# One step of a hybrid decoder layer: the attention's query tile, softmax maxima and head norm, written with other instructions

## Chip, cores and metric

The kernel runs on one core of one Trainium2 chip. The metric is the device time of one execution in microseconds, as the median of several runs, lower being better. The engines are called PE (TensorE; PEld are its weight loads), DVE (VectorE), ACT (ScalarE), POOL (GpSimd) and SP (SyncE, used only to issue DMAs).

## The reference, cut to what matters

The layer has two parts that read the same normalised input: differential attention (4 heads, each with two query/key halves of 64 and values of 128) and a gating MLP over chunks of 128 positions. Their results are concatenated, projected and added to the input; then comes a feed-forward network with 4096 hidden channels. It does this for a prompt of 512 tokens and for 8 sequences of 4 new tokens each, which read 4096 cached positions through a page table.

```python
def prompt_diff_attn(q, k, v, lam):          # per block of 128 queries
    s = einsum('bthcd,bshcd->bhcts', q_blk, k) * QK_DIM ** -0.5
    p = softmax(where(causal, s, -inf), axis=-1)
    a = p[:, :, 0] - lam * p[:, :, 1]        # the two halves of a head
    return einsum('bhts,bshd->bthd', a, v)

def merge_out(att, mix, subln_gain, lam_init, w_out):
    o_att = (rms_norm(att, subln_gain) * (1.0 - lam_init)).reshape(B, T, ATT_WIDTH)
    return concatenate([o_att, mix], axis=-1) @ w_out

def sample_diff_attn(q, k_new, v_new, k_past, v_past, lam):
    # the same softmax difference, over 4096 cached positions and the new ones
```

All tensors are fp32. rms_norm divides each row by the root of its mean square and multiplies it with a gain vector; for the attention's result that gain, `subln_gain`, has one entry for each of the 128 value channels and is the same for all heads.

## The kernel before, in words

Tokens lie on partitions in four tiles of 128 (the 32 new tokens are a fifth, small one), or on columns where a matmul needs them so. To keep fp32 accuracy each weight block and each activation is split into a rounded part and the rest (`wh`/`wl`, `Thi`/`Tlo`), and each product is three matmuls. `w_conv` (line 262) splits a weight block: ScalarE rounds, VectorE subtracts; `split` (line 716) does the same for a transposed activation tile.

The work is a main line, with two streams beside it. The main line is `setup`, `in_proj` (line 821: ten column blocks of the input projection), `out_proj` (line 1052) and eight groups of the feed-forward network (`ffn`, line 1141). The first stream is the new tokens' attention over the cache: 64 steps, each with one indirect DMA of keys (`kraw`), a 32x32-block transposition of them on VectorE (`k_tr`, line 557, tile `kt`), scores (`scores`, line 573, PSUM tile `S`), a softmax, transposed probabilities copied out by ScalarE (`ptr`, line 614, tile `PT`) and a product with the cached values (PSUM tile `O`). Eight steps are one sequence, so `scores` starts a new sequence every eighth step. `pump` (line 692) sets these steps out along the main line by costs that the main line reports. The second stream is the prompt's attention, 16 units of (query tile i, head h) in three stages: `attn_a` (line 952) computes scores and the unnormalised difference of the two softmaxes, `attn_b` transposes it, `attn_c` (line 1003) multiplies with the values. Its stages are interleaved with the later column blocks of `in_proj` and the first of `out_proj`.

The order of instructions on an engine isn't quite that of the program: the framework orders them by its own estimates, and the class `Ordered` (line 41) bounds this. In the stretches called `pinned` every engine keeps the program's order. Outside them VectorE and TensorE may move an instruction by up to 28 places, GpSimd not at all, and ScalarE and SP freely. Then each engine runs its list in order.

The places that the change touches:

- `qz_fill` (line 566) fills the tile `qz`, the stationary operand of the new tokens' scores. It has four blocks of 32 partitions, one for each of four positions in a page, and in block q only the columns of q may differ from zero; the rest was set to zero once. It is filled once for a sequence by eight copies of 32x32 out of `qT4`, which lies on partitions 64 to 95 of the tile `rows`. The first matmul of a sequence's scores waits for it, and the next fill waits for the last scores of the sequence before.
- `masks` makes `mh`, a 128x4 tile that is 1 where a partition belongs to block q; it is there before the first fill.
- `attn_a` finds the maximum over the keys of each of the two score tiles, multiplies both maxima with minus 1/8, and takes the exponentials with that bias and a scale of 1/8. `tr_pair` (line 730), which writes the transposed queries, multiplies with a column of the queries' gain out of `gcol`; `finish_piece` (line 746) calls it.
- `attn_c` scales a head's result on ScalarE. After the fourth head it forms the norm's factor on GpSimd, and then multiplies each head's 128x128 block in place with that factor and with `sg`, the gain times 0.8 spread over all partitions.
- `cat_tile` (line 1024) transposes four such blocks, so that channels lie on partitions, and calls `split`.
- `gcols` (line 488) turns a small tile with gain rows into the columns `gcol`; `setup` (line 392) loads its rows through SP.

Of the kernel before, what the change touches and what calls it, by code (L numbers as in the profile page):

```python
# [62 lines left out]
def kernel(  # L63
# [114 lines left out]
    idxK = const.tile([128, NCH], I32, name="idxK")  # L178
    gcol = const.tile([128, 32], F32, name="gcol")
    bhalf = const.tile([128, 4], F32, name="bhalf")  # L180
    wT = const.tile([128, 4, 128], F32, name="wT")
    wTs = const.tile([32, 4, 32], F32, name="wTs")
    bsr = const.tile([32, 20], F32, name="bsr")
# [9 lines left out]
    neglam = const.tile([128, 1], F32, name="neglam")  # L193
    lt = gg[:, 0:256]
    lamsgn = const.tile([64, 1], F32, name="lamsgn")
    qz = const.tile([128, 16, 32], F32, name="qz")

    spk = smp.tile([128, 8, 64], F32R, tag="spk", name="spk")
    cs = []
# [192 lines left out]
    def setup():  # L392
        kt0 = kvp.tile([128, 4096], F32, tag="kt", name="kt0")
        xs = kt0[0:32, 0:1024]
        gm = kvp.tile([128, 1024], F32, tag="pp", name="gm")
        fg = kvp.tile([128, 2048], F32, tag="v", name="fg", bufs=VB)
        junk = kvp.tile([128, 512], F32, tag="om", name="junk")
        ptb = zt_().bitcast(I32).rearrange("p (n q) -> p n q", q=4)
        F = fg[:, 0:896].rearrange("p (f m) -> p f m", f=7)
        gsrc = fg[:, 896:1024]  # L400
        SP.dma_start(out=xs, in_=xs_d)
        SP.dma_start(out=ptb, in_=page_table.rearrange("b l -> (b l)").unsqueeze(0).to_broadcast([128, 256]).rearrange("p (n q) -> p n q", q=4))
        SP.dma_start(out=gm, in_=norm_mix.to_broadcast([128, 1024]))
        w_issue()
        w_issue()
        SP.dma_start(out=xt[0], in_=xp[:, 0, :])
        for o in (1024, 3072):
            w_issue(kt0[:, o:o + 1024].rearrange("p (k c) -> p k c", k=4))
        SP.dma_start(out=qg, in_=q_gain.to_broadcast([128, 64]))
        for t in range(1, 4):  # L410
            SP.dma_start(out=xt[t], in_=xp[:, t, :])

        G.memset(mhalf, -0.5)
        for t in ssb + [cst]:
            G.memset(t, 1.0)
        kw = dict(base=0, channel_multiplier=0, allow_small_or_imprecise_dtypes=True)
        G.iota(pf[:, 7:8], pattern=[[0, 1]], base=0, channel_multiplier=1, allow_small_or_imprecise_dtypes=True)
        make_identity(nc, idt)
        G.iota(F[:, 0].rearrange("p (a b) -> p a b", b=32), pattern=[[0, 4], [1, 32]], **kw)
        G.iota(F[:, 1].rearrange("p (a b) -> p a b", b=32), pattern=[[1, 4], [0, 32]], **kw)  # L420
        G.iota(F[:, 2].rearrange("p (a b) -> p a b", b=8), pattern=[[0, 16], [1, 8]], **kw)
        G.iota(F[:, 3].rearrange("p (a b c) -> p a b c", b=4, c=8), pattern=[[0, 4], [1, 4], [0, 8]], **kw)
        G.iota(F[:, 4].rearrange("p (a b c) -> p a b c", b=8, c=4), pattern=[[0, 4], [1, 8], [0, 4]], **kw)
        G.iota(F[:, 5], pattern=[[1, 128]], **kw)
        G.iota(F[:, 6].rearrange("p (a b) -> p a b", b=4), pattern=[[0, 32], [1, 4]], **kw)
        G.memset(gsrc[0:32, :], 0.0)


        pinned(True)
        for half in range(2):  # L430
            ps = dt_()
            n = 4 if half == 0 else 1
            for i in range(n):
                PE.transpose(ps[:, 128 * i:128 * i + 128], F[:, 4 * half + i], idt)
            V.tensor_copy(out=pf[:, 4 * half:4 * half + n], in_=ps.rearrange("p (f m) -> p f m", f=4)[:, 0:n, 0])

        keep_warm(8)

        x_stat(4, [xs], 32, junk, G)
        xsg = kt0[0:32, 2048:3072]  # L440
        V.tensor_tensor(out=xsg, in0=xs, in1=gm[0:32], op=ALU.mult)
        w_conv()
        ps = dt_()
        for k in range(8):
            PE.transpose(ps[:, 32 * k:32 * k + 32], xsg[:, 128 * k:128 * k + 128], idt[:32, :32])
        keep_warm(5)
        pack(ps[:, 0:256].rearrange("p (k t) -> p k t", k=8), 0, 8)
        w_conv()

        for q in range(4):  # L450
            V.tensor_scalar(out=idxK[32 * q:32 * q + 32, :], in0=ptb[32 * q:32 * q + 32, :, q], scalar1=32.0,
                            scalar2=pf[32 * q:32 * q + 32, 0:1], op0=ALU.mult, op1=ALU.add)
        x_gain(gm, 0)
        for n in range(KB):
            gK(n)
        w_conv()
        SP.dma_start(out=gsrc[0:8, :], in_=norm_mix.rearrange("a (k p) -> (a k) p", p=128))
        SP.dma_start(out=gsrc[8:16, :], in_=norm_ffn.rearrange("a (k p) -> (a k) p", p=128))
        SP.dma_start(out=gsrc[16:20, :], in_=b_spatial.rearrange("a g t -> (a g) t"))
        SP.dma_start(out=gsrc[20:21, 0:64], in_=q_gain)  # L460
        SP.dma_start(out=gsrc[20:21, 64:128], in_=q_gain)
        G.memset(qz, 0.0)
        G.memset(strip, 0.0)
        G.memset(ones, 1.0)
        causal = zt_()[:, 0:128]
        G.memset(causal, 0.0)
        G.affine_select(out=causal, in_=causal, pattern=[[-1, 128]], compare_op=ALU.is_ge, fill=NEG, base=0,
                        channel_multiplier=1)
        G.tensor_copy(out=cab, in_=causal)
        G.tensor_copy(out=idb, in_=idt)  # L470
        return gm, F, gsrc, junk
# [16 lines left out]
    def gcols(gsrc):  # L488
        ps = dt_()
        PE.transpose(ps[:, 0:32], gsrc[0:32, 0:128], idt[:32, :32])  # L490
        V.tensor_copy(out=gcol, in_=ps[:, 0:32])

    def load_params():
        for i, lv in enumerate((lambda_q1, lambda_q2, lambda_k1, lambda_k2)):
# [69 lines left out]
        gK(n + KB)  # L564

    def qz_fill(b):
        for q in range(4):
            for c in range(2):
                V.tensor_copy(
                    out=qz[32 * q:32 * q + 32].rearrange("p (h x e) m -> p h x e m", x=2, e=2)[:, :, c, :, 8 * q + 4 * c:8 * q + 4 * c + 4],  # L570
                    in_=qT4.rearrange("p (h x e) m -> p h x e m", x=2, e=2)[:, :, c, :, 4 * b:4 * b + 4])

    def scores(m):
        b, pj = divmod(m, 4)
        if pj == 0:
            qz_fill(b)
        if pj % 2 == 0:
            Sb[b, pj // 2] = psx.tile([128, 512], F32, tag="S", name="S", bufs=2)
        S = Sb[b, pj // 2]
        kt = ktp.pop(m)  # L580
        for s in range(4):
            for h in range(4):
                mm(S[32 * h:32 * h + 32, 256 * (pj % 2):256 * (pj % 2) + 256].rearrange("p (j x) -> p j x", j=2),
                   qz[:, 4 * h + s, :], kt[:, :, 4 * h + s].rearrange("p j i s -> p j (i s)"), s == 0, s == 3)

    def sm1(b):

# [125 lines left out]
                PE.transpose(ps[:, 128 * k:128 * k + 128], xg[t % 2][:, 128 * kk:128 * kk + 128], idt)  # L713
            split(ps.rearrange("p (k t) -> p k t", k=4), 4 * hf, t)

    def split(psv, k0, t):
        hi = Thi[:, k0:k0 + 4, 128 * t:128 * t + 128]
        A.copy(out=hi, in_=psv)
        V.tensor_tensor(out=Tlo[:, k0:k0 + 4, 128 * t:128 * t + 128], in0=psv, in1=hi, op=ALU.subtract)

    def optB(ps, t, hiw, low, half, first=0):

# [23 lines left out]
    def finish_piece(kind, p, ss, items):  # L746
# [18 lines left out]
        def tr(i):  # L765
            z, n, t = items[i]
            if kind == "g":
                return
            dst = (qT if kind == "q" else kT)[:, 2 * p:2 * p + 2, 128 * t:128 * t + 128] if t < 4 else \
                kTs[:, 2 * p:2 * p + 2, :]  # L770
            tr_pair(z, n, dst, gcol[:, 20:21] if kind == "q" else None)

        later(stat)
        for i in range(len(items)):
# [177 lines left out]
    def attn_a(i, h):  # L952
# [7 lines left out]
        a = st_()  # L960
        P = [tt_(), tt_()]
        for c in range(2):
            V.tensor_reduce(out=a[:, c:c + 1], in_=S[c][:, 0:nk], axis=AX.X, op=ALU.max)
        V.tensor_scalar(out=a[:, 0:2], in0=a[:, 0:2], scalar1=-SCALE, scalar2=None, op0=ALU.mult)
        for c in range(2):
            A.activation(out=P[c][:, 0:nk], in_=S[c][:, 0:nk], func=ACTF.Exp, bias=a[:, c:c + 1], scale=SCALE,
                         accum_out=a[:, 2 + c:3 + c])
        V.reciprocal(out=a[:, 4:6], in_=a[:, 2:4])
        V.scalar_tensor_tensor(out=a[:, 3:4], in0=a[:, 5:6], scalar=neglam, in1=a[:, 2:3], op0=ALU.mult, op1=ALU.mult)
# [33 lines left out]
    def attn_c(i, h):  # L1003
# [11 lines left out]
        if h == 3:  # L1015
            rsqrt(ss[:, 0:4], EPS, 1.0 / 128.0)

            def go():
                for j in range(4):
                    V.scalar_tensor_tensor(out=cat[:, j, :], in0=cat[:, j, :], scalar=ss[:, j:j + 1], in1=sg,  # L1020
                                           op0=ALU.mult, op1=ALU.mult)
            later(go)

    def cat_tile(i, k0s=(0, 4)):

        srcs = [qT[:, k, 128 * i:128 * i + 128] for k in range(4)] + \
            [mix[0][:, i, 128 * k:128 * k + 128] for k in range(4)]
        for k0 in k0s:
            ps = dt_()
            for k in range(4):  # L1030
                PE.transpose(ps[:, 128 * k:128 * k + 128], srcs[k0 + k], idt)
            split(ps.rearrange("p (k t) -> p k t", k=4), k0, i)

    def attention():
        units = [(i, h) for i in range(4) for h in range(4)]
# [370 lines left out]
```

## Time and profile before

| | us |
|---|---|
| median of 3 runs | 833.59 |
| lowest and highest | 831.65, 834.48 |
| the profiled execution | 832.81 |
| its span, first to last instruction | 831.1 |
| PE busy | 804.0 (97%) |
| DVE busy | 545.5 (66%) |
| ACT busy | 357.4 (43%) |
| POOL busy | 187.1 (23%) |

The mean granted clock of PE over the span was 0.986 of full speed. DMAs moved 219.06 MB at 264 GB/s. The first 36 us are setup; the input projection and both attentions fill the time to about 366 us; from there the feed-forward network runs with the rest of the cache stream beside it, to about 600 us, and then alone with the new tokens' part.

A row names the engine, the operation, the tile written and the tiles read, the shape as partitions x elements of a partition, and how often it occurs. "Idle before" is time in which the engine stood still just before these instructions, with the instruction that ended it. Since the ends of matmuls are modelled, a stretch in which PE is busy throughout may still hold small gaps; the share of weight loads (PEld) shows them better. All names have one line, L52, because every operation goes through one helper.

### The profile page before, as it was taken

To read this page: it belongs to the slowest core of one execution; us is meant where nothing else is said; L and a number is where in the kernel's file an instruction comes from. 1 tells how busy PE (TensorE), PEld (TensorE's weight loads), DVE (VectorE), ACT (ScalarE), POOL (GpSimd) and SP (SyncE) were. 2 spreads that over 40 slices of the span, in tenths; PEclk is the share of its full clock that TensorE was granted. 3 is DMA by queue.
4 is the path that set the end of the run, shared out by engine and by line. 5 is a ranking of instruction groups with operands and counts; after the bars stand their busy time and mean duration, and the time that the engine had idled before them with its cause. 6 is when DMAs were issued, how large, how long until landed. Compare 5 with 4: busy or idle time off the path is not lost.

```text
span 831.1 us, 15443 instructions
## 1 busy us (share of the span) xinstructions
PE 804.0 (97%) x6210; PEld 636.0 (77%) x6210; DVE 545.5 (66%) x957; ACT 357.4 (43%) x888; POOL 187.1 (23%) x196
## 2 busy tenths in 40 slices
PE   5899999999899999989999999999999999999997
PEld 5888887766556788876766767666776898998997
DVE  5878866888988954797777676644744534444354
ACT  4544643766563743645154144163332431331231
POOL 4553542254333312222322132120100000000000
PEclk8799999999999999999999999999999999999999
DMA  8597698896978888867989797784597277576202
GB/s 316 194 377 270 229 350 323 301 332 260 366 267 311 339 304 317 324 244 289 337 338 345 290 359 305 259 341 167 171 291 247 80 244 244 172 234 221 76 14 95
DMA packets 101797, 219.06 MB, mean 264 GB/s; under 512 B 6089, under 2 KB 83997, under 8 KB 85341
## 3 DMA queue, kind: packets, MB, share of 16 engines
q0 software_dynamic: 18432, 134.23, 42.1%
q1 hardware_dynamic: 83292, 83.84, 30.7%
q8 instruction: 49, 0.80, 0.4%
q14 instruction: 24, 0.19, 0.1%
HBM read 213.53 MB, written 4.52 MB: 262 GB/s over the span
## 4 chain that ended last, share of the span: by engine, by line
PE 79%; DVE 9%; ACT 6%; DMA 3%; issue 2%; POOL 0%; SPq 0%; DVEq 0%; ACTq 0%
PE d L52 68%; PE O L52 6%; PE S L52 6%; DVE kt L52 3%; ACT PT L52 2%; DMA raw<-in_w_down_dram 1%; DMA kraw<-in_cache_k_dram,idxK 1%; DVE zn L52 1%; DMA raw<-in_w_in_dram 1%; ACT wh L52 1%; DVE Tlo L52 1%; DVE wl L52 1%; ACT t L52 1%; ACT z L52 1%; DVE s L52 1%
## 5 line engine op out<-in xcount | busy, mean ns | idle before, releaser
L52 ACT CAST wh<-raw 128x1024 fp32r<-128x1024 f32 x90 | 94.1, 1048 | 198.5 <-PE d L52 179.0
L52 PE MATMUL d<-a,wh 128*128 128x272 f32 (+1 forms) x704 | 167.0, 341 | 0.0
L52 DVE STREAM_TRANSPOSE kt<-kraw 128x2048 f32<-128x2048 f32 x64 | 146.4, 2297 | 11.2 <-PE S L52 7.7
L52 DVE TENSOR_TENSOR wl<-raw,wh 128x1024 fp32r<-128x1024 f32 x90 | 109.4, 1218 | 57.1 <-ACT wh L52 56.9
L52 PEld LDWEIGHTS d<-a,wh 128*128 128x128 f32 x704 | 113.1, 188 | 24.6 <-issue 5.4
L52 PE MATMUL d<-wh,Thi 128*128 128x256 f32 x432 | 129.0, 299 | 1.8 <-ACT d L52 1.0
L52 POOL DMA_INDIRECT v<-in_cache_v_dram,idxK x64 | 67.0, 1047 | 255.0 <-PE O L52 244.5
L52 PE MATMUL d<-wl,Thi 128*128 128x256 f32 x432 | 123.4, 286 | 0.0
L52 PE MATMUL d<-wh,Tlo 128*128 128x256 f32 x432 | 122.5, 284 | 0.0
L52 PE MATMUL d<-Thi,wh 128*128 128x272 f32 (+2 forms) x368 | 108.7, 336 | 0.0
L52 PE MATMUL d<-Tlo,wh 128*128 128x272 f32 (+2 forms) x368 | 106.5, 330 | 1.4 <-DVE Tlo L52 1.4
L52 PE MATMUL d<-Thi,wl 128*128 128x272 f32 (+2 forms) x368 | 106.4, 329 | 0.0
L52 PE MATMUL d<-a,wl 128*128 128x272 f32 (+1 forms) x352 | 102.8, 336 | 0.0
L52 POOL DMA_INDIRECT kraw<-in_cache_k_dram,idxK x64 | 73.8, 1153 | 110.6 <-DVE kt L52 63.6
L52 PEld LDWEIGHTS d<-wh,Thi 128*128 128x128 f32 x432 | 82.8, 192 | 11.6 <-issue 6.9
L52 PEld LDWEIGHTS d<-wh,Tlo 128*128 128x128 f32 x432 | 82.7, 192 | 0.5 <-issue 0.4
L52 PEld LDWEIGHTS d<-wl,Thi 128*128 128x128 f32 x432 | 82.7, 191 | 0.1
L52 PEld LDWEIGHTS d<-Thi,wh 128*128 128x128 f32 x368 | 63.5, 188 | 18.2 <-issue 7.5
L52 ACT COPY PT<-d 32x128 f32<-32x128 f32 x256 | 65.7, 257 | 14.3 <-DVE d L52 11.1
L52 PEld LDWEIGHTS d<-Tlo,wh 128*128 128x128 f32 x368 | 63.6, 188 | 7.4 <-DVE Tlo L52 1.6
L52 PEld LDWEIGHTS d<-Thi,wl 128*128 128x128 f32 x368 | 63.5, 188 | 6.2
L52 PEld LDWEIGHTS d<-a,wl 128*128 128x128 f32 x352 | 60.1, 188 | 7.0
(265 smaller groups left out, 1080.3 us busy)
## 6 DMA issues: line engine op xcount, KB each, us to landing
raw<-in_w_up_dram SPq DMA_DIRECT2D x32, 512.0 KB
raw<-in_w_down_dram SPq DMA_DIRECT2D x32, 512.0 KB
plain<-in_w_up_dram SPq DMA_DIRECT2D x20, 512.0 KB
plain<-in_w_down_dram SPq DMA_DIRECT2D x20, 512.0 KB
raw<-in_w_in_dram SPq DMA_DIRECT2D x18, 512.0 KB
raw<-in_w_out_dram SPq DMA_DIRECT2D x8, 512.0 KB
plain<-in_w_out_dram SPq DMA_DIRECT2D x8, 512.0 KB
r<-in_x_prompt_dram SPq DMA_DIRECT2D x4, 512.0 KB
```

The costliest lines, as they stand in the source:

```text
L52: r = f(*args, **kw)
```

## The change

Four edits, all of which keep the result the same up to rounding:

- The query tile. At the first sequence ScalarE copies the queries of all sequences, four times, into a new tile `qrep` on all 128 partitions. Each fill then is two products (one for each query half) of `qrep`, spread over the four blocks, with the mask `mh`, spread over positions; they write the zeros too. The tile's columns are ordered by query half first.
- The maxima. The reduction writes the negated maximum, and the scaling behind it goes. The factor 1/8 is put into the queries' gain column (`qcol`), so that scores come out scaled and the exponentials have a scale of 1.
- The heads' norm. One product with the factor spread over the channels takes the place of four with factor and gain. The gain times 0.8 (`sgcol`, a column, from one more gain row that SP loads) is applied in `split`, after the transposition, by ScalarE's scale and by a three-operand form of VectorE's subtraction.
- `gcols` makes the two new columns, by two short scalings.

```diff
+    qcol = const.tile([128, 1], F32, name="qcol")
+    sgcol = const.tile([128, 1], F32, name="sgcol")
...
-    qz = const.tile([128, 16, 32], F32, name="qz")
+    qz = const.tile([128, 2, 8, 32], F32, name="qz")
+    qrep = const.tile([128, 2, 8, 32], F32, name="qrep")
...
         SP.dma_start(out=gsrc[20:21, 64:128], in_=q_gain)
+        SP.dma_start(out=gsrc[21:22, :], in_=subln_gain)
...
         V.tensor_copy(out=gcol, in_=ps[:, 0:32])
+        V.tensor_scalar(out=qcol, in0=gcol[:, 20:21], scalar1=SCALE, scalar2=None, op0=ALU.mult)
+        V.tensor_scalar(out=sgcol, in0=gcol[:, 21:22], scalar1=1.0 - LAM_INIT, scalar2=None, op0=ALU.mult)
...
     def qz_fill(b):
-        for q in range(4):
-            for c in range(2):
-                V.tensor_copy(
-                    out=qz[32 * q:32 * q + 32].rearrange("p (h x e) m -> p h x e m", x=2, e=2)[:, :, c, :, 8 * q + 4 * c:8 * q + 4 * c + 4],
-                    in_=qT4.rearrange("p (h x e) m -> p h x e m", x=2, e=2)[:, :, c, :, 4 * b:4 * b + 4])
+
+        if b == 0:
+            for q in range(4):
+                A.copy(out=qrep[32 * q:32 * q + 32].rearrange("p x (h e) m -> p h x e m", h=4),
+                       in_=qT4.rearrange("p (h x e) m -> p h x e m", x=2, e=2))
+        for c in range(2):
+            V.tensor_tensor(out=qz[:, c].rearrange("p f (q c t) -> p f q c t", c=2, t=4)[:, :, :, c, :],
+                            in0=qrep[:, c, :, 4 * b:4 * b + 4].unsqueeze(2).to_broadcast([128, 8, 4, 4]),
+                            in1=mh.unsqueeze(1).unsqueeze(3).to_broadcast([128, 8, 4, 4]), op=ALU.mult)
...
-                   qz[:, 4 * h + s, :], kt[:, :, 4 * h + s].rearrange("p j i s -> p j (i s)"), s == 0, s == 3)
+                   qz[:, s // 2, 2 * h + s % 2, :], kt[:, :, 4 * h + s].rearrange("p j i s -> p j (i s)"), s == 0, s == 3)
...
-    def split(psv, k0, t):
+    def split(psv, k0, t, col=None):
         hi = Thi[:, k0:k0 + 4, 128 * t:128 * t + 128]
-        A.copy(out=hi, in_=psv)
-        V.tensor_tensor(out=Tlo[:, k0:k0 + 4, 128 * t:128 * t + 128], in0=psv, in1=hi, op=ALU.subtract)
+        lo = Tlo[:, k0:k0 + 4, 128 * t:128 * t + 128]
+        if col is None:
+            A.copy(out=hi, in_=psv)
+            V.tensor_tensor(out=lo, in0=psv, in1=hi, op=ALU.subtract)
+        else:
+            A.activation(out=hi, in_=psv, func=ACTF.Copy, scale=col)
+            V.scalar_tensor_tensor(out=lo, in0=psv, scalar=col, in1=hi, op0=ALU.mult, op1=ALU.subtract)
...
-            tr_pair(z, n, dst, gcol[:, 20:21] if kind == "q" else None)
+            tr_pair(z, n, dst, qcol if kind == "q" else None)
...
         for c in range(2):
-            V.tensor_reduce(out=a[:, c:c + 1], in_=S[c][:, 0:nk], axis=AX.X, op=ALU.max)
-        V.tensor_scalar(out=a[:, 0:2], in0=a[:, 0:2], scalar1=-SCALE, scalar2=None, op0=ALU.mult)
+            V.tensor_reduce(out=a[:, c:c + 1], in_=S[c][:, 0:nk], axis=AX.X, op=ALU.max, negate=True)
         for c in range(2):
-            A.activation(out=P[c][:, 0:nk], in_=S[c][:, 0:nk], func=ACTF.Exp, bias=a[:, c:c + 1], scale=SCALE,
+            A.activation(out=P[c][:, 0:nk], in_=S[c][:, 0:nk], func=ACTF.Exp, bias=a[:, c:c + 1], scale=1.0,
...
-                for j in range(4):
-                    V.scalar_tensor_tensor(out=cat[:, j, :], in0=cat[:, j, :], scalar=ss[:, j:j + 1], in1=sg,
-                                           op0=ALU.mult, op1=ALU.mult)
+                V.tensor_tensor(out=cat, in0=cat, in1=ss[:, 0:4].unsqueeze(2).to_broadcast([128, 4, 128]), op=ALU.mult)
...
-            split(ps.rearrange("p (k t) -> p k t", k=4), k0, i)
+            split(ps.rearrange("p (k t) -> p k t", k=4), k0, i, None if k0 else sgcol)
```

## Rows read from the trace of the kernel before

**Rows 1.** The page's busy us by engine (share of the span) x instructions.

```profile
PE 804.0 (97%) x6210; PEld 636.0 (77%) x6210; DVE 545.5 (66%) x957; ACT 357.4 (43%) x888; POOL 187.1 (23%) x196
```

**Rows 2.** Busy us by stage; after POOL come granted clock, DMA share, GB/s.

```profile
36.00:366.00 330.00, 318.75 (x2840) 252.60 (x2841) 260.93 (x521) 181.08 (x525) 117.56 (x107) 0.99 0.84 309
140.00:300.00 160.00, 152.48 (x1316) 106.73 (x1315) 139.71 (x306) 100.16 (x318) 57.33 (x54) 1.00 0.82 306
300.00:340.00 40.00, 40.00 (x371) 35.35 (x370) 23.51 (x28) 13.60 (x30) 9.52 (x13) 1.00 0.91 329
366.00:580.00 214.00, 214.00 (x1320) 145.66 (x1320) 141.35 (x182) 82.69 (x186) 48.62 (x46) 1.00 0.80 300
```

**Rows 3.** Waits of TensorE from 36 to 365 us: total us, times, longest.

```profile
PE d L52 <- ACT PT L52: 2.7, 3, 1.3
PE d L52 <- ACT t L52: 0.5, 1, 0.5
```

**Rows 4.** VectorE's groups by form: xcount | busy us, mean ns | idle before.

```profile
L52 DVE COPY qz<-rows 32x32 f32<-32x32 f32 x64 | 9.8, 187 | 0.9
L52 DVE TENSOR_TENSOR z<-d,maskn 64x128 f32<-64x128 f32 x1 | 0.3, 283 | 0.1
L52 DVE TENSOR_SCALAR s<-s 128x2 f32<-128x2 f32 x16 | 2.5, 154 | 0.1
L52 DVE SCALAR_TENSOR_TENSOR r<-r,s,sg 128x128 f32<-128x128 f32 x16 | 4.5, 340 | 0.0
L52 DVE TENSOR_TENSOR r<-r,t 128x512 f32<-128x512 f32 x4 | 2.5, 687 | 1.2 <-ACT t L52 1.2
L52 DVE TENSOR_TENSOR Tlo<-d,Thi 128x512 fp32r<-128x512 f32 x16 | 10.7, 681 | 0.8 <-issue 0.4 <-ACT Thi L52 0.2
L52 DVE SCALAR_TENSOR_TENSOR Tlo<-mix,gcol,Thi 128x512 fp32r<-128x512 f32 x2 | 1.4, 732 | 0.0
```

**Rows 5.** ScalarE's groups by form.

```profile
L52 ACT COPY t<-osum 32x512 f32<-32x512 f32 x1 | 0.6, 621 | 0.0
L52 ACT ACTIVATE r<-d,gcol 128x256 f32<-128x256 f32 x8 | 3.3, 470 | 1.0 <-PE d L52 1.0
L52 ACT COPY r<-d 128x256 f32<-128x256 f32 x8 | 2.8, 380 | 0.7 <-PE d L52 0.6
```

**Rows 6.** Timeline round the first fill: start us, us, what [idle before].

```profile
36.70 0.42 PE L52 MATMUL d<-idt,zn 32*128 32x32 f32 x2 [1.93 <-ACT z L52]
40.03 0.81 DVE L52 COPY qz<-rows 32x32 f32<-32x32 f32 x6
42.79 1.05 ACT L52 CAST wh<-raw 128x1024 fp32r<-128x1024 f32 x1 [5.42 <-PE d L52]
43.71 1.93 PE L52 MATMUL S<-kt,qz 128*32 128x256 f32 x32
```

**Rows 7.** Timeline of SP's queue where the gain rows are loaded.

```profile
16.27 1.46 SPq L52 DMA_DIRECT2D fg<-in_q_gain_dram  x2
18.76 0.40 SPq L52 DMA_DIRECT2D raw<-in_w_in_dram  x1
```

**Rows 8.** Pieces of the chain that ended last: start us, us, what.

```profile
85.14 0.43 DVE qz L52 x2
...
133.09 0.09 DVE s L52
...
208.22 1.02 DVE r L52 x4
...
252.27 1.05 DVE r L52 x4
...
255.19 2.22 DVE kt L52
257.41 0.06 DVE s L52
```

**Rows 9.** Busy us and granted clock from 36 to 44 us.

```profile
36.00:44.00 8.00, 7.30 (x40) 6.73 (x44) 5.34 (x15) 2.17 (x6) 4.45 (x7) 0.57 0.73 262
```

## The prediction, made before the changed kernel had run

> **What bounds the kernel now.** I read the page's busy times first, then a table of busy time by stage, then TensorE's waits in the stage where it waits, and last the chain of waits. TensorE is busy 804.0 of 831.1 us, VectorE 545.5 [rows 1]. By stage this splits. From 366 to 580 us TensorE is busy 214.00 of 214.00 us, so there VectorE can give nothing back. From 36 to 366 us, where projection, prompt attention and the first cache pages run together, TensorE is busy 318.75 of 330: it stands still for 11.25 us. In the middle of it, from 140 to 300 us, VectorE is busy 139.71 of 160, the highest share it has anywhere, and weight loads fill 106.73 of 160 us, 67%, against 35.35 of 40, 88%, from 300 to 340 us, where nothing waits [rows 2]. So the room is in this stage: 11.25 us that are plainly idle, and more in thin stretches that the modelled ends of matmuls cover. Of TensorE's own waits there the largest of nine groups is for ScalarE's copies into PT, 2.7 us, and 0.5 us are for one exponential [rows 3].
>
> **The change part by part.** All times are of one profiled execution, 832.81 us with a span of 831.1; the median of the runs is 833.59, 0.78 above. I work out a difference and take it from the median.
>
> The query tile. Removed are 64 copies of 32x32, 9.8 us busy, 153 ns each (187 mean, they overlap). Added are 16 products of 128x128; the trace has no product with two spread operands. The nearest row is a two-input product of 128 columns at 283 ns, so 16 x 283 = 4.5 us. One product for a copy's price (153) gives 2.4; four times the copy, for four times the columns, 9.8. I take 4.5, since the 283 is for the same operation and width. VectorE: minus 5.3 us [rows 4]. First what the rows show: a copy of 32 columns takes 187 ns and a product of 128 takes 283, so most of a short instruction is not its columns [rows 4]. The Trainium skill (VectorE: DVE Perf Modes, section The perf-mode tier table) speaks against this edit: an fp32 copy within SBUF runs at two elements a cycle, an fp32 tensor_tensor at one. By columns alone a fill would go from 8 x 16 = 128 cycles to 2 x 128 = 256, 0.13 us more at the page's 0.96 GHz, 1.1 us over eight fills where I have 5.3 less; the rows decide.
>
> At the first fill ScalarE also gets four copies of 32x512. The row for that shape is 621 ns, 2.5 us in all [rows 5]. I cost them at nothing on the path: ScalarE idles 5.42 us before its conversion at 42.79 us, so from 37.4; four copies end near 40, the old fill began at 40.03, and the first scores began only at 43.71 [rows 6]. Without that cover they cost what the rival below says.
>
> The maxima. Removed are 16 scalings of 128x2, 2.5 us at 154 ns [rows 4]. A negating reduction is shown nowhere; I take it at the plain one's time, since the shape is the same, with one more scaling's 154 ns as its dearest, which would cancel this edit.
>
> The heads' norm. Four times, four products of 128x128 (16 in all, 4.5 us busy) become one of 128x512. Its row is 687 ns, 2.7 us, minus 1.8. At the split the subtraction becomes the three-operand form: 732 for 681 ns, four times, plus 0.2 [rows 4]. On ScalarE a scale read per partition costs 470 against 380 ns, plus 0.09 four times [rows 5]. The two constants are two short scalings on VectorE, 0.3 us at the price of the scaling above. The added load of a gain row goes onto SP's queue, 0.73 us like its two neighbours; the next load there left SP 1.0 us after they ended, so it is delayed by nothing [rows 7].
>
> Together VectorE loses 5.3 + 2.5 + 1.8 - 0.2 - 0.3 = 9.1 us of 545.5. What of this lies on the path is read from the chain. Copies of the tile stand on it in two places, 0.43 at 85.14 and later one copy more, 0.60 in all; at 4.5/9.8 of their time that is 0.3 saved. The norm's groups of four stand on it twice, 1.02 and 1.05; at 0.69 each, 0.7 saved. The scaling stands on it four times with 0.09 to 0.06, 0.3 in all. The last of them is the telling one: after the second maximum was found, a transposition of keys, 2.22 us, ran before the scaling at 257.41, and the exponentials waited behind both [rows 8]. With no scaling, they can start when the second maximum is done. At the least this saves the wait that TensorE shows there, 0.5 us [rows 3]; at the most the 2.22. I take the middle, 1.4, because the stage's weight loads show that TensorE is less full than its busy time says. Sum: 0.3 + 0.7 + 0.3 + 1.4 = 2.7 us, with bounds of 1.8 and 3.5. The median goes to 833.59 - 2.7 = **830.9 us**, 0.32% less. What is late next are ScalarE's copies into PT, which nothing here shortens.
>
> **The rivals.**
>
> First, nothing reaches the end. TensorE's largest wait in the stage is named after ScalarE [rows 3], ScalarE's work grows by 2.9 us, and the order of instructions is found anew at build time, so that a transposition may stand before another short instruction instead. Against it: the norm's groups and the transposition are on the chain itself [rows 8]. Time: between 832.5 and 834, 833.3.
>
> Second, VectorE is the bound of the stage from 140 to 300 us. For it speak its 87% there and the thin weight loads [rows 2]. Then all that it sheds in this stretch comes off: three fills (3 x 0.66 = 2.0 us), some twelve scalings (1.9) and the norm (1.8), 5.7 us, and 827.9 us. Against it: TensorE's largest wait names ScalarE. The Trainium skill (Trainium Kernel Development and Optimization, section Best Practices) says to judge the distance to the limit by weight-load time and not by matmul time; the stage's 67% against 88% agrees that there is more room than 11.25 us.
>
> Third, on the other side: the first fill is late. Its products need all four copies on ScalarE, and these are issued in the program behind a conversion that waits until 42.79 us [rows 6]. If they are placed behind it, they run from 43.84 to 46.3, the products end at 46.9, and the scores start 3.2 us later than 43.71; VectorE, in order, stands behind the products too. An idle TensorE can then lose its clock: after 1.93 us of standing still before 36.70 [rows 6] it was granted 0.57 on average from 36 to 44 us, most of that at the lower of its two levels, 1.2 and 2.4 GHz, which is 0.43 x 8 = 3.4 us of full clock lost [rows 9]. Price 3.2 + 3.4 = 6.6, on top of the forecast 837.5 us. It decides from the point where the last copy ends later than about 43.2 us.
>
> Fourth, the change does not do what it says: the products with spread operands cost four copies each (upper bound) and the negating reduction a scaling more. Then only the norm's 0.7 and half of the transposition are left, 832.2 to 833.
>
> **How the numbers follow.** A measurement of this kernel can tell some 0.3%, 2.5 us, from no change. The forecast (gain 1.8 to 3.5) has 0.42, of which some 0.30 lies beyond 2.5 us; VectorE as the bound 0.12; nothing reaches the end 0.23; the change that does less than it says 0.05; the late fill 0.14, and another placing that loses as much 0.04. Faster: 0.30 + 0.12 = 0.42. Slower: 0.18. Within: 0.40, with the forecast's lower part. The forecast's own range is 830.1 to 831.8. The whole range must take in the second rival with 1.5 us for what it leaves out, and reach the third: 826.4 to 837.5, with about 0.1 left out at each end.
>
> **What would show it.** Right: VectorE some 9 us below 545.5; products on the query tile near 283 ns; the reductions unchanged at their widths; one product of about 690 ns per query tile for the norm; the exponentials of the units at 255 us starting right behind the second maximum; idle time of TensorE from 36 to 366 us below 11.25 by 1 to 2 us; nothing changed from 366 us on except that it all lies earlier. Wrong: four copies on ScalarE that end after 43 us and a gap before the first scores with a low clock behind it; waits of TensorE in the stage that only change their names, from VectorE to ScalarE; or a stage that ends at 366 us as before although VectorE lost its 9 us.

## The result, and the profile after

The changed kernel takes 824.74 us (median of 5 runs, 822.46 to 827.14), the one before 833.93: a ratio of 0.990, 95% interval 0.9876 to 0.9924. It is 9.2 us faster where 2.7 were forecast, and it lies 1.7 us below the range's lower end. The profiled execution took 822.46 us. Of the seven runs of e15_m1h (under Halving the transposition) two fell in a slower state, 852 and 1555 us, and its figures are those of the other five.

The page of the changed kernel, busy us by engine; it answers to [rows 1]:

```profile
PE 797.2 (97%) x6210; PEld 632.2 (77%) x6210; DVE 536.3 (65%) x883; ACT 359.9 (44%) x892; POOL 181.6 (22%) x196
```

VectorE lost 9.2 us, as worked out (9.1). TensorE has the same 6210 matmuls and is 6.8 us less busy, although nothing in the change shortens a matmul.

The stages of the changed kernel (columns as in [rows 2]). The first stage ends 11 us earlier here, so its row goes to 355, and the stage of the feed-forward part begins there:

```profile
36.00:355.00 319.00, 312.52 (x2841) 249.46 (x2842) 253.18 (x458) 183.31 (x528) 112.76 (x107) 1.00 0.87 321
129.00:289.00 160.00, 157.16 (x1383) 113.45 (x1382) 139.06 (x276) 105.34 (x332) 52.53 (x54) 1.00 0.87 327
355.00:569.00 214.00, 214.00 (x1321) 145.79 (x1321) 139.84 (x170) 82.63 (x186) 48.29 (x46) 1.00 0.81 299
36.00:44.00 8.00, 7.50 (x75) 6.15 (x76) 6.85 (x11) 4.75 (x10) 4.55 (x7) 1.00 0.77 297
```

The stage of 214 us behind it is as full as before, and the matmul on z and ones that ends the first stage starts at 352.8 us instead of 363.9: the whole gain of this execution, 11.1 us, less 0.7 given back behind it, lies in the first stage. There TensorE, with the same number of matmuls (2841, 2840 before), stands still for 319.00 - 312.52 = 6.5 us instead of 11.25, and is busy for 6.2 us less.

About half of those 6.2 us is not the change. In the profile of before the granted clock was 0.57 from 36 to 44 us [rows 9] and it is 1.00 here, so the matmuls ahead of the new tokens' first scores took longer there. From the first scores on (43.71 us before, 40.34 after) the rows are, before and after (columns as in [rows 2]):

```profile
43.71:366.00 322.29, 311.74 (x2809) 246.07 (x2809) 255.72 (x507) 179.19 (x521) 113.40 (x101) 1.00 0.84 310
40.34:355.00 314.66, 308.69 (x2814) 246.05 (x2814) 249.14 (x452) 180.28 (x521) 111.02 (x104) 1.00 0.87 322
```

That is 7.6 us less, of which 4.6 are idle time of TensorE and 3.0 busy time. So the busy share hid some 3 us of room, as the thin weight loads had said. VectorE is as full as before from 129 to 289 us (139.06 of 160; 139.71 before): it did not become idler, the work went by faster (TensorE does 1383 matmuls there, 1316 before).

TensorE's waits in that stage (total us, times, longest), answering to [rows 3]:

```profile
PE d L52 <- ACT z L52: 2.5, 2, 1.9
PE d L52 <- DVE Tlo L52: 2.0, 3, 1.4
PE d L52 <- ACT PT L52: 1.4, 3, 0.7
```

The wait for ScalarE's copies into PT halved, from 2.7 us, though nothing in the change shortens a copy.

VectorE's and ScalarE's edited groups in the changed kernel (columns as in [rows 4]):

```profile
L52 DVE TENSOR_TENSOR qz<-qrep,mh 128x128 f32<-128x128 f32 x16 | 4.2, 283 | 0.0
L52 DVE TENSOR_REDUCE s<-d 128x1 f32<-128x512 f32 x8 | 5.3, 679 | 2.3 <-PE d L52 2.3
L52 DVE TENSOR_REDUCE s<-d 128x1 f32<-128x128 f32 x8 | 2.0, 282 | 1.2 <-PE d L52 1.1
L52 DVE TENSOR_TENSOR r<-r,s 128x512 f32<-128x512 f32 x4 | 2.6, 660 | 0.0
L52 DVE SCALAR_TENSOR_TENSOR Tlo<-d,sgcol,Thi 128x512 fp32r<-128x512 f32 x4 | 3.0, 746 | 0.0
...
L52 ACT ACTIVATE Thi<-d,sgcol 128x512 fp32r<-128x512 f32 x4 | 2.7, 680 | 0.0
L52 ACT COPY qrep<-rows 32x512 f32<-32x512 f32 x4 | 2.5, 617 | 0.1
```

The prices held: products 283 ns (283 taken), norm 660 (687), split 746 (732). A negating reduction costs what a plain one did, 679 and 282 ns now for 684 and 276 before:

```profile
L52 DVE TENSOR_REDUCE s<-d 128x1 f32<-128x512 f32 x8 | 5.4, 684 | 0.9 <-PE d L52 0.8
L52 DVE TENSOR_REDUCE s<-d 128x1 f32<-128x128 f32 x8 | 2.0, 276 | 0.1
```

Where a unit's time went is read from one unit of four blocks in both kernels. VectorE and ScalarE, kernel before:

```profile
241.04 0.69 DVE L52 TENSOR_REDUCE s<-d 128x1 f32<-128x512 f32 x1
242.55 0.69 DVE L52 TENSOR_REDUCE s<-d 128x1 f32<-128x512 f32 x1 [0.81 <-PE d L52]
243.16 2.30 DVE L52 STREAM_TRANSPOSE kt<-kraw 128x2048 f32<-128x2048 f32 x1
245.38 0.13 DVE L52 TENSOR_SCALAR s<-s 128x2 f32<-128x2 f32 x1
...
248.29 2.31 DVE L52 STREAM_TRANSPOSE kt<-kraw 128x2048 f32<-128x2048 f32 x1
251.01 0.74 DVE L52 SCALAR_TENSOR_TENSOR t<-t,s 128x512 f32<-128x512 f32 x1
...
245.75 1.04 ACT L52 CAST wh<-raw 128x1024 fp32r<-128x1024 f32 x1 [0.58 <-PE d L52]
246.70 0.68 ACT L52 ACTIVATE t<-d,s 128x512 f32<-128x512 f32 x1
```

And the same unit after:

```profile
231.28 0.69 DVE L52 TENSOR_REDUCE s<-d 128x1 f32<-128x512 f32 x1
232.91 0.69 DVE L52 TENSOR_REDUCE s<-d 128x1 f32<-128x512 f32 x1 [0.94 <-PE d L52]
233.51 2.30 DVE L52 STREAM_TRANSPOSE kt<-kraw 128x2048 f32<-128x2048 f32 x1
236.35 0.75 DVE L52 SCALAR_TENSOR_TENSOR t<-t,s 128x512 f32<-128x512 f32 x1
...
232.01 0.69 ACT L52 ACTIVATE t<-d,s 128x512 f32<-128x512 f32 x1 [0.47 <-DVE s L52]
233.69 0.69 ACT L52 ACTIVATE t<-d,s 128x512 f32<-128x512 f32 x1 [0.91 <-DVE s L52]
```

Before, the one scaling for both maxima stood behind a key transposition of 2.30 us. ScalarE had meanwhile been given a conversion of 1.04 us, the exponentials followed at 246.70, and the difference (t<-t,s) stood behind the next transposition: from the first maximum to its end 251.75 - 241.04 = 10.7 us. After, the first exponential runs before the second maximum is found, both are over while the transposition runs, and the same path takes 237.10 - 231.28 = 5.8. Over the 16 units, the time from the end of the second maximum to the start of the first exponential adds up to 20.4 us before and to -5.2 after (below zero, since a first exponential now mostly starts before the second maximum is found); the number of key transpositions that stand between a unit's second maximum and its difference goes from 10 to 3.

### The profile page after: what moved, and what is told of

It reads as the page before. It is cut to its first block, busy times and chain, and to the rows that moved or that the text cites. A ratio compares the mean times of both kernels' runs of the same rounds, so it can differ in the third digit from the quotient of the medians.

```text
span 820.7 us, 15362 instructions
## 1 busy us (share of the span) xinstructions
PE 797.2 (97%) x6210; PEld 632.2 (77%) x6210; DVE 536.3 (65%) x883; ACT 359.9 (44%) x892; POOL 181.6 (22%) x196
## 4 chain that ended last, share of the span: by engine, by line
PE 73%; DVE 10%; DMA 7%; ACT 5%; issue 2%; POOL 1%; SPq 0%; DVEq 0%; ACTq 0%; POOLq 0%
PE d L52 63%; PE O L52 5%; DMA kraw<-in_cache_k_dram,idxK 5%; PE S L52 5%; DVE kt L52 4%; ACT PT L52 2%; DMA raw<-in_w_down_dram 1%; DVE zn L52 1%; DMA kt<-in_w_in_dram 1%; DVE Tlo L52 1%; ACT z L52 1%; ACT wh L52 1%; ACT t L52 1%; DVE wl L52 1%; POOL ssb L52 0%
## 5 line engine op out<-in xcount | busy, mean ns | idle before, releaser
L52 DVE STREAM_TRANSPOSE kt<-kraw 128x2048 f32<-128x2048 f32 x64 | 146.3, 2297 | 12.4 <-PE S L52 7.5
L52 POOL DMA_INDIRECT kraw<-in_cache_k_dram,idxK x64 | 70.8, 1107 | 102.3 <-DVE kt L52 54.6
```

What stands on the lines that cost most here:

```text
L52: r = f(*args, **kw)
```

## The experiments

Each kernel is measured against runs of the kernel before on the same chip, whose median was 833.07 us (first four), 831.97 (next four), 833.14 (next four) and 832.75 (last three).

**The parts alone, and VectorE's time put back.** The first three apply one of the edits each, with the constant that it needs. e4_pad is the changed kernel with 16 reductions over wT whose results nobody reads:

```diff
+    scr = const.tile([128, 1], F32, name="scr")
...
+        V.tensor_reduce(out=scr, in_=wT.rearrange("p g t -> p (g t)")[:, 0:384], axis=AX.X, op=ALU.max)
         aux["a", i, h] = P[0]
```

Expected of e1_max:

> The edit of the maxima alone, on the kernel before: negating reductions, no scaling, the factor 1/8 in the queries' gain. Theory wait (the exponentials of the prompt's attention stood behind key transpositions that ran between the second maximum and its scaling; that wait is the gain of some 8 us from 130 to 250 us): this edit alone brings most of it, 826 to 828 us, and idle time of ScalarE for the bias shrinks. Theory time (VectorE's busy time bounds the stage, and each part gives what it sheds there): it sheds 2.5 - 0.2 us, so 831.5. Theory order (what counts is the new order that the build finds, not an edit): any value from 822 to 836, and the three parts do not add up.

Expected of e2_norm:

> The edit of the heads' norm alone: one product for four, the gain at the split. Theory wait: it shortens a row of short instructions that stands on the chain twice, 833.9 - 0.7 = 833.2. Theory time: it sheds 1.8 - 0.2 - 0.2 us, so 832.5. Theory order: any value, and the parts do not add up.

Expected of e3_fill:

> The edit of the query tile alone: two products for eight copies. Theory wait: it touches no exponential; it can bring the 3 us that the changed kernel won before 100 us, so 830.5 to 831.5. Theory time: it sheds 4.0 us from 36 to 366 us, so 829.9. Theory order: any value. If the early 3 us come from the fill, the first scores start near 40.3 us here as in the changed kernel, against 43.7; if they come from the clock alone, they do not, or only in runs with a clock above 0.995.

Expected of e4_pad:

> The changed kernel with 16 more reductions of 128x384 on VectorE, one behind each attention unit, whose result nobody reads: at 546 ns each 8.7 us, about what the change sheds. Theory wait: the exponentials don't wait for them by program order, so the gain stays but for an instruction that now and then stands behind one: 825 to 828. Theory time: all of the gain from 130 to 250 us goes, 832 to 834. Theory order: any value.

| kernel | median us | ratio, 95% interval | VectorE busy us |
|---|---|---|---|
| e1_max | 829.16 | 0.9947 (0.9931 to 0.9964) | 544.6 |
| e2_norm | 833.0 | 1.0019 (1.0000 to 1.0038) | 544.6 |
| e3_fill | 830.37 | 0.9968 (0.9957 to 0.9980) | 537.7 |
| e4_pad | 827.37 | 0.9930 (0.9917 to 0.9943) | 541.9 |

The parts add up to 3.9 + 0.1 + 2.7 = 6.7 us, 2.5 less than the whole; by the ratios it is 0.66% against 1.0%. The maxima alone gave more than all that had been forecast, but less than the theory of the wait had it (826 to 828). The norm's and the tile's times lie between the theories and decide nothing. The padding's reductions take 8.6 us, which makes VectorE's busy time, overlaps counted once, 541.9 - 536.3 = 5.6 us longer, and give back about 2.6 us of the 9.2. So a microsecond of VectorE counts for 0.3 to 0.5 here, and its 9.2 us for no more than half of the gain.

**What about the maxima costs?** Four kernels. e5_two scales each maximum by itself, right behind it; e6_act gives the joint scaling to ScalarE; e7_joint is the changed kernel with a copy that makes both exponentials wait for both maxima again; e8_nf is the whole change without the maxima.

```diff
 e5_two (in the loop over c)
+            V.tensor_scalar(out=a[:, c:c + 1], in0=a[:, c:c + 1], scalar1=-SCALE, scalar2=None, op0=ALU.mult)
-        V.tensor_scalar(out=a[:, 0:2], in0=a[:, 0:2], scalar1=-SCALE, scalar2=None, op0=ALU.mult)
 e6_act
-        V.tensor_scalar(out=a[:, 0:2], in0=a[:, 0:2], scalar1=-SCALE, scalar2=None, op0=ALU.mult)
+        A.mul(out=a[:, 0:2], in_=a[:, 0:2], mul=-SCALE)
 e7_joint (the exponentials take bias=a[:, 6 + c:7 + c])
+        A.copy(out=a[:, 6:8], in_=a[:, 0:2])
```

Expected of e5_two:

> The kernel before with two scalings of 128x1 in place of the one of 128x2: each right behind its own maximum, so that the first exponential needs neither the second maximum nor what VectorE is given between. VectorE does not less but 16 short instructions more, about 2 us. Theory 'wait' (the first exponential waited for both maxima and for VectorE's list between them): the 20.4 us that stood between the second maximum's end and the first exponential over the 16 units fall to 0 or below, the stretch from the first to the last mask product falls from 131.2 us by 3 to 5, and the time is 828 to 831. Theory 'time' (only VectorE's time counts, 0.3 us for each us, as the padding showed): 833.5 to 834. Theory 'order' (any edit redraws VectorE's list, by chance): anywhere from 829 to 836, with the 20.4 us no guide to it.

Expected of e6_act:

> The kernel before with the one scaling of both maxima moved from VectorE to ScalarE: VectorE gets rid of 16 instructions, 2.5 us, no transposition can stand before the scaling, but both exponentials still wait for the second maximum. Theory 'wait', in its form that VectorE's list between the maximum and the exponential is what cost: the 20.4 us fall to 16 times a scaling of ScalarE and its hand-over, 5 to 8 us, and the time is 829 to 831.5. In its form that waiting for the second maximum is what cost: 832 to 833.5. Theory 'time': 832.3 (2.5 us x 0.3). Theory 'order': no relation.

Expected of e7_joint:

> The changed kernel with one ScalarE copy of both negated maxima ahead of the exponentials, which take their bias from the copy: all of the change stays, VectorE does exactly as much, and only the early start of the first exponential is taken away (16 short instructions more on ScalarE, which is busy 44%). Theory 'wait for the second maximum': gives back most of the gain of the maxima, time 827.5 to 830. Theory 'VectorE's list between' or 'time': little is given back, 824.7 to 826.5.

Expected of e8_nf:

> The query tile and the norm together, the maxima as before. If the parts add, 833.1 - 2.7 (tile alone) - 0 (norm alone) = 830.4. Theory 'wait' says that what the three parts give together beyond their sum (2.8 us) needs the maxima: 830 to 831 here. Theory 'time' (VectorE sheds 7 us, at 0.3 us for each): 831. If the tile and the norm are those that help one another: 827 to 828.5.

| kernel | median us | ratio, 95% interval | maximum to exponential, 16 units |
|---|---|---|---|
| e5_two | 828.89 | 0.9958 (0.9945 to 0.9972) | 2.5 us |
| e6_act | 827.34 | 0.9950 (0.9933 to 0.9967) | 9.0 |
| e7_joint | 824.16 | 0.9903 (0.9889 to 0.9918) | 9.5 |
| e8_nf | 829.94 | 0.9974 (0.9964 to 0.9985) | 18.4 |

e7_joint gives nothing back (0.9903 against 0.990): that the first exponential waited for the second maximum did not cost anything at the end. e6_act says what did: with the same joint wait, and only the scaling taken out of VectorE's list, 4.6 us are gained (0.33 to 0.67% by the interval, 2.7 to 5.6 us), of which the 2.5 us of VectorE's time can be 0.8 to 1.2 at the padding's rate. e5_two adds 16 instructions to VectorE and still gains 3.1, which the theory of VectorE's time alone (833.5 to 834) excludes. Three ways of getting the joint scaling out of VectorE's list (negated maxima, a scaling for each, ScalarE) give 3.9, 3.1 and 4.6 us, with intervals that overlap. The sum of the waits came out longer than expected in both (2.5 us for 0 or below, 9.0 for 5 to 8), and e6_act faster than expected. e8_nf sheds nearly all of the time and gains little:

```profile
PE 801.6 (97%) x6210; PEld 634.8 (77%) x6210; DVE 536.8 (65%) x898; ACT 359.8 (43%) x892; POOL 184.3 (22%) x196
```

8.7 of VectorE's 545.5 us are gone here, and 2.0 of the kernel's. By itself this fits the theory of VectorE's time (0.3 for each) as well as that of the wait.

**Pairs, and a control of the order.** e9_mf is the maxima with the tile, e10_mn the maxima with the norm. The controls change one constant of the kernel before and of the changed one:

```diff
-WINDOW = 28
+WINDOW = 32
```

Expected of e9_mf:

> The maxima and the query tile together, the norm as before. Singly they gave 0.53% and 0.32%, the whole change 1.0%. If these two add and the norm is the one that gains from them: 0.85% off, 826. If the tile needs the maxima (VectorE's short work counts only when the exponentials no longer wait for its list) and the norm is worth nothing: 1.0% off, 824.5. If order decides: between 824 and 829 with no relation to either.

Expected of e10_mn:

> The maxima and the norm together, the query tile as before. If the norm is worth nothing with the maxima too: 0.5% off, 828.5 to 829. If it gains with them what the sum lacks: 0.7 to 0.8% off, 826.5. With the pair of maxima and tile, this says which part the extra 2.8 us hang on.

Expected of e11_bw:

> A control: the kernel before with 32 in place of 28 as the number of places within which VectorE and TensorE may be given work out of turn. No work is removed or added; only the order in which the engines are given it is drawn anew. Theory 'order' (any redrawing moves the time by some tenths of a per cent either way): 0.3% or more away from 832.5. Theory 'wait' or 'time': within 0.2%, 831 to 834.

Expected of e12_aw:

> The same control on the changed kernel: 32 places in place of 28. Theory 'order': 0.3% or more away from 824.7, and more likely slower than faster if the changed kernel's order was a lucky one. Theory 'wait' or 'time': within 0.2%, 823 to 826.5.

| kernel | median us | ratio, 95% interval |
|---|---|---|
| e9_mf | 827.64 | 0.9925 (0.9898 to 0.9953) |
| e10_mn | 824.21 | 0.9891 (0.9869 to 0.9913) |
| e11_bw | 832.09 | 0.9991 (0.9976 to 1.0006) |
| e12_aw | 823.47 | 0.9880 (0.9857 to 0.9902) |

The controls move by 0.1 and 0.2%, so these two new orders are not worth 1% by themselves; others were not tried. They hardly touch the units: 17.3 us for 20.4 stand between maxima and exponentials in e11_bw, -4.8 for -5.2 in e12_aw. e9_mf, with 5.5 us and a wide interval, comes to less than the two parts added (826 was expected) and shows no sign of holding what the sum lacks. The pair without the tile is as fast as the whole change, although the page of e10_mn shows VectorE hardly relieved:

```profile
PE 798.0 (97%) x6210; PEld 632.4 (77%) x6210; DVE 543.1 (66%) x931; ACT 357.6 (44%) x888; POOL 182.3 (22%) x196
```

2.4 us less on VectorE go with 8.9 us less in the end; in e8_nf it was 8.7 with 2.0. So the time that VectorE sheds does not set the gain. And the norm, worth nothing alone, is worth 829.16 to 824.21, 5 us, beside the maxima. The trace of e1_max shows where it lacks them (VectorE, then TensorE):

```profile
203.57 2.30 DVE L52 STREAM_TRANSPOSE kt<-kraw 128x2048 f32<-128x2048 f32 x1
...
205.84 2.29 DVE L52 STREAM_TRANSPOSE kt<-kraw 128x2048 f32<-128x2048 f32 x1
208.27 0.62 DVE L52 SCALAR_TENSOR_TENSOR t<-t,s 128x384 f32<-128x384 f32 x1
210.72 0.71 DVE L52 COPY qz<-rows 32x32 f32<-32x32 f32 x5
213.43 0.17 DVE L52 COPY qz<-rows 32x32 f32<-32x32 f32 x1
...
212.17 1.07 PE L52 MATMUL S<-kt,qz 128*32 128x256 f32 x16
213.06 1.02 PE L52 MATMUL O<-v,PT 128*32 128x512 f32 x2
213.66 1.07 PE L52 MATMUL S<-kt,qz 128*32 128x256 f32 x15
```

And its stretches from 230 us on (columns as in [rows 2]):

```profile
230.00:240.00 10.00, 8.93 (x45) 5.94 (x43) 6.37 (x9) 7.41 (x26) 1.53 (x2) 0.78 0.97 358
240.00:250.00 10.00, 10.00 (x90) 6.99 (x89) 8.12 (x15) 4.49 (x12) 4.34 (x6) 0.88 0.65 190
```

And of e10_mn in the same place:

```profile
204.24 2.30 DVE L52 STREAM_TRANSPOSE kt<-kraw 128x2048 f32<-128x2048 f32 x1
206.95 0.61 DVE L52 SCALAR_TENSOR_TENSOR t<-t,s 128x384 f32<-128x384 f32 x1
207.57 1.04 DVE L52 COPY qz<-rows 32x32 f32<-32x32 f32 x7
...
210.01 0.17 DVE L52 COPY qz<-rows 32x32 f32<-32x32 f32 x1
...
208.90 1.07 PE L52 MATMUL S<-kt,qz 128*32 128x256 f32 x16
210.24 1.07 PE L52 MATMUL S<-kt,qz 128*32 128x256 f32 x16 [0.28 <-DVE qz L52]
```

With the maxima alone a second transposition got in front of a unit's difference at 208.27, the next fill's copies ended at 213.60 instead of 210.18, and the scores of the cache page came in pieces among O's matmuls. TensorE shows as busy in that stretch. Then TensorE was granted its lower level, 1.2 GHz, for part of 230 to 250 us (means of 0.78 and 0.88), after it had stood still 1.08 us at 218.4 and 0.77 at 232.3; e10_mn has 1.00 there. That is 0.22 x 10 + 0.12 x 10 = 3.4 us of full clock lost in this execution. That the norm's shorter work moved that transposition is read from these two traces; no run moved it alone. Nor is the clock all of the 5 us: the three runs of e1_max with a mean clock of 0.991 or more took 826.7, 827.4 and 829.5 us, the five such runs of e10_mn 823.4 to 824.6.

**Halving the transposition.** The same data are transposed in two instructions of 128x1024, so that short work can stand between them. Made of the kernel before (e13_bh), of the changed one (e14_ah) and of the maxima alone (e15_m1h):

```diff
-        V.transpose(out=ktp[m][:, jj].rearrange("p f i s -> p i f s"),
-                    in_=kr.pop(n).rearrange("p (i f d) -> p i f d", i=4, f=16))
+        kw = kr.pop(n).rearrange("p (i f d) -> p i f d", i=4, f=16)
+        ko = ktp[m][:, jj].rearrange("p f i s -> p i f s")
+        for u in range(0, 4, 2):
+            V.transpose(out=ko[:, u:u + 2], in_=kw[:, u:u + 2])
```

Expected of e13_bh:

> The kernel before with each of the 64 key transpositions (128x2048, 2.3 us) as two halves of 128x1024, between which VectorE can be given short work; no work is removed, and 64 instructions of some 0.1 us fixed cost are added. Theory 'place' (what cost before were short instructions of the attention's chain behind a transposition of 2.3 us): none can be held up by more than 1.2 us unless both halves stand together, so 0.4 to 0.9% faster than before, 825.5 to 830. Theory 'time': VectorE has 4 to 6 us more, at 0.3 us for each 1.2 to 1.8 us slower, 834 to 835.

Expected of e14_ah:

> The changed kernel with the same halves. Theory 'place': little is left to gain, 823 to 826.5, and the distance to the kernel before with halves is 1 to 4 us instead of 9. Theory 'time': 825.5 to 827, the distance stays 8 to 9.

Expected of e15_m1h:

> The maxima alone with the same halves. Theory 'place': what the norm gave with the maxima (4.9 us) came from two transpositions in a row before a difference at 204 us; with halves the maxima alone come to 824 to 827. Theory 'time': 830 to 831.

e13_bh took 827.86 us, 0.9949 (0.9930 to 0.9968); e14_ah 822.05, 0.9877 (0.9854 to 0.9901); e15_m1h has a ratio of 0.9929 (0.9905 to 0.9952), against 0.9947 without halves. The page of e13_bh:

```profile
PE 800.2 (97%) x6210; PEld 633.8 (77%) x6210; DVE 549.0 (66%) x1021; ACT 357.8 (43%) x888; POOL 181.3 (22%) x196
```

And the group of transpositions before, and of halves in e13_bh (columns as in [rows 4]):

```profile
L52 DVE STREAM_TRANSPOSE kt<-kraw 128x2048 f32<-128x2048 f32 x64 | 146.4, 2297 | 11.2 <-PE S L52 7.7 <-DMA kraw<-in_cache_k_dram,idxK 3.2
L52 DVE STREAM_TRANSPOSE kt<-kraw 128x1024 f32<-128x1024 f32 x128 | 152.8, 1222 | 10.4 <-PE S L52 6.9 <-DMA kraw<-in_cache_k_dram,idxK 3.2
```

VectorE does 3.5 us more, nothing of the change is in it, and 4.9 us are gained: what its longest block holds up counts here, and not how much it does. What it holds up isn't located by this. The scalings are a small part: 18.4 of the 20.4 us between maxima and exponentials are still there in e13_bh. The distance between the kernel before and the changed one shrinks from 9.2 to 5.8 us, to less than "time" had it (8 to 9) and more than "place" had it (1 to 4). So the transposition's place carries a part, not all. e15_m1h misses what "place" had said: the halves give the maxima alone 0.2%, with intervals that overlap, where the norm gives them 0.6%. So the transposition in front of the difference at 208 us is not shown to be what the norm took away. e14_ah lies below every other kernel here, but its interval meets that of the change; that it is faster isn't shown.

## Why the prediction was wrong

**The bound and VectorE's sum: right.** The gain lies in the first stage alone, and VectorE's 9.1 us came out as 9.2, each price within 30 ns.

**The failed step: the transposition between the second maximum and the scaling, 1.4 us (0.5 to 2.2).** The mechanism was seen and sized at one place, the one that the chain of waits shows. The chain is the path of one execution and shows each delay only where it ended last. In VectorE's own list, over all 16 units, three transpositions stood between a second maximum and its scaling and seven more between the scaling and the difference. Taking the scaling out of the list by itself measured 4.6 us (e6_act; 3.9 as in the change, e1_max), without any other edit; the term and the four scalings (0.3) were 1.7. The middle between 0.5 and 2.2 was chosen for thin weight loads; they would have justified looking at every unit.

**Adding pieces of the chain failed too.** The norm's 0.7 measured nothing alone and 5 us beside the maxima; the fills' 0.3 measured 2.7 alone and nothing on top of maxima and norm. The sum of 2.7 took the three for independent. Of the 6.5 us that it missed, some 2 are the maxima, 2 the fills less the norm, and 2.5 what the edits give only together. That each edit moves transpositions in VectorE's list, so that its worth hangs on the others, is the likely reason, but it is read from the traces and no run shows it; why the fills alone give 2.7 stays open too.

**The rivals.** VectorE as the bound (827.9) came nearest in time, but its reason does not hold: the time came off without VectorE being relieved (e10_mn, e13_bh), and came off little where it was (e8_nf). Nothing reaching the end and a change that does less than it says fell with the result. The late first fill did not occur: ScalarE's four copies ended at 39.03, before the old fill had begun (40.03).

The first fill in the changed kernel (timeline, ScalarE, VectorE, TensorE), answering to [rows 6]:

```profile
36.42 0.62 ACT L52 COPY qrep<-rows 32x512 f32<-32x512 f32 x1
37.16 1.87 ACT L52 COPY qrep<-rows 32x512 f32<-32x512 f32 x3
...
39.56 0.48 DVE L52 TENSOR_TENSOR qz<-qrep,mh 128x128 f32<-128x128 f32 x2
...
36.34 0.31 PE L52 MATMUL d<-idt,zn 32*128 32x32 f32 x2 [1.93 <-ACT z L52]
40.34 1.93 PE L52 MATMUL S<-kt,qz 128*32 128x256 f32 x32
```

The scores start 3.4 us earlier than at 43.71. This was in no term of the sum. It is mostly the clock: after the same 1.93 us of standing still TensorE was granted 1.00 from 36 to 44 us, where the profile of before had 0.57 [rows 9]; e2_norm, e5_two and e6_act, with the old fill and 1.00 there, start their scores at 40.9, 40.7 and 40.6. The new fill's own part is what is left, 0.2 to 0.5 us. The mean clock also differs between runs of one kernel, and the time with it: of 64 runs of the kernel before, the 41 with a mean clock of 0.985 to 0.988 have a median of 833.0 us, the 13 with 0.992 or more 831.0. Of e6_act's nine runs four at 0.986 to 0.988 took 829.5 to 829.8 and four at 0.993 to 0.998 took 825.3 to 825.9, so its median, 827.34, is the one run between. The changed kernel's five runs have 0.987 to 0.998. So the two profiles lie some 3 us further apart at their start than the edits account for, and the clock may hold up to 2 of the 9.2 us. Compared at like clock 7 to 8 us are left: 825.4 for 833.0 in the one run at 0.987, and a median of 823.9 for 831.0 in the three at 0.993 or more. That is still far beyond 2.7.

**By its own signs.** The exponentials start behind their own maximum, products and reductions are as forecast, and from the end of the first stage on nothing changed. TensorE's idle time fell by 4.8 us and not by 1 to 2, and from the first scores on another 3.0 came off in busy time. So there was more to gain than the forecast had.

**What stays open.** Why e7_joint is as fast as the change with 9.5 us between maxima and exponentials: the sum over the units is a sign, not the measure. The transpositions don't order the times either: in e7_joint seven stand between the second maxima and the differences, as many as in e5_two, and in e1_max four, though e7_joint is the fastest of the three. So the scaling's cost is shown as a whole, by kernels with and without it, and not wait by wait. And whether the low clock of e1_max at 230 us is in all its executions; one was profiled. e5_two and e8_nf have such a fall too, near 223 us, so part of what separates these profiles from the change's may be the clock; no run separates the two.

## What to carry to other kernels

On an engine with a list in order, a short instruction can cost as much as the longest block that stands before it: count, over all units and not only on the chain, how often that happens, and take the instruction off that list or cut the block. Removing a short instruction that others wait for can be worth more than its own duration (here about 4 us for 16 scalings of 2.5 us in all), and halving the longest block can beat removing work (here 4.9 us with 3.5 us more of VectorE, against 2.0 us with 8.7 less). Where edits redraw an order, measure them together, since their gains need not add.

## What the runs showed of the hardware

A two-input product takes 283 ns at 128 columns, with operands spread by a stride of zero (qz) as without (z) [rows 4], and 660 at 512 with one operand spread. That is 377 ns for 384 columns more, so by an estimate some 126 of the 283 are columns and 157 fixed. Halves of a 2297 ns transposition took 1222 each, 147 more for the pair. The Trainium skill (VectorE: DVE Perf Modes, section The TRN2 errata) has a fixed cost per instruction for operands in SBUF, about 150 cycles as measured there, by an estimate 156 ns at its 0.96 GHz; these runs agree.

The mean granted clock differs between runs of one kernel, and the time with it, by 2 us in the 64 runs above and by 4 in e6_act's. Between profiles the difference lies mostly at the start (0.57 and 1.00 from 36 to 44 us); the clock also fell in the middle, to a mean of 0.78 from 230 to 240 us in e1_max and to 0.83 from 220 to 230 us in e5_two and e8_nf. The Trainium skill (TensorE: Matmul & The Clock Gate, section What's actually happening) calls the start of a kernel variable from run to run; the profiles of kernels that do the same work up to there agree (0.57 before, 0.79 in e11_bw).
